# The end of a gradient kernel that is bound by transfers: the last tile's load without a wait and in one piece, its result in four pieces

## Chip, cores, metric

The kernel runs on one core of a Trainium2 chip. The metric is the device time of one execution in microseconds (us), the median of several runs. The profile is that of one execution; its span is some 2 us shorter than the time.

## The reference

```python
def setup_inputs():
    return {"x": np.random.randn(8192, 8192).astype(np.float32)}

def reference(x):
    return np.gradient(x, axis=1)
```

Inside a row every result is half the difference of the two neighbours; at the two ends it is the one-sided difference. 268.44 MB are read and as much is written.

## The kernel before

A tile is 256 rows: 128 partitions with two rows (R = 2) of 8192 values each, 64 KB per partition, 8.39 MB in all. There are 32 tiles (numbers 0 to 31) and three slots (NB = 3) for them. SP issues the loads, ScalarE the stores of tiles 0 to 30, SP the two stores of tile 31. GpSimd saves the end differences, VectorE computes in place (the result lies 64 values to the left of the input in the same slot), VectorE or ScalarE puts the ends in.

```python
def load(i):
    k = i % NB
    if i < NB:
        parts = [(ld[k], 0, R)]
    else:
        nc.sync.wait_ge(ld[(i - 1) % NB], 16 * ld_n[(i - 1) % NB])   # the load in front
        nc.sync.wait_ge(st[k], 16 * st_n[k])                         # the slot is free
        parts = [(ld[k], 0, R)] if i < nsets - 1 else [(ld_rows[r], r, 1) for r in range(R)]
    for sem, r0, nr in parts:
        nc.sync.dma_start(
            out=slots[k][:, SH + r0 * m : SH + (r0 + nr) * m],
            in_=x_sets[i, :, r0 * m : (r0 + nr) * m],
        ).then_inc(sem, 16)
    ld_n[k] += 1
...                                                                  # put_aside, work: cut
for i in range(NB):
    load(i)
for i in range(nsets):
    k = i % NB
    if i < nsets - 1:
        ready = put_aside(i, 0, R, ld[k], 16 * ld_n[k])
        placer = nc.scalar if i % 2 else nc.vector
        work(i, 0, R, ready, placer, nc.scalar, st[k])
        st_n[k] += 1
    else:                                                            # the last tile, row by row
        for r in range(R):
            ready = put_aside(i, r, 1, ld_rows[r], 16)
            work(i, r, 1, ready, nc.vector, nc.sync, st_rows[r])
    if i + NB < nsets:
        load(i + NB)
```

## Time and profile before

| | before |
|---|---|
| time, first three runs | 1249.37 us (1248.43 to 1249.98) |
| span of the profiled execution | 1246.3 us |
| bytes moved | 536.87 MB |
| VectorE busy | 554.4 us, 44% |
| the 16 DMA engines | busy without a hole until the last packets |

The page cuts the span into 40 slices; in each, the DMA row gives the busy share of the DMA engines in tenths and the row below it their rate. A transfer consists of packets, which the trace records one by one with queue, size, start and duration. Here a packet is one contiguous run of one partition: 65,536 bytes for a full tile (128 packets, eight on each engine, 2.418 us each), 32,768 bytes for one row (1.213 us). The records do not name the engine, but their number in flight at any moment does for this argument: 16 means that all engines work (the mean from 4 to 1242 us is 16.0). At the end of each transfer come 16 packets of 4 bytes, which I call the reports of the engines (1056 of them for the 66 transfers of this profile). The engine that waits for a tile goes on some 0.4 us after the last of the 16 (tile 30: reports from 1172.1 to 1176.1, GpSimd at 1176.5; second row of tile 31: last report at 1222.2, GpSimd at 1222.6). Queue q1 is SP's, q10 is ScalarE's. The lines themselves are in the prediction below.

One correction to it in advance: the times that the prediction reads from packet records (not those from the profile's own views) are 0.24 us too late, because I aligned the two clocks by hand. One reading is off by more: the first of the 16 engines is through at 1242.3, not at 1242.9, so the last packets end over 2.0 us and not over 1.7.

### The profile page before, as it was taken

Reading aid. Unit: us, or ns where it says so; the run is one execution under the profiler, and the core shown is the slowest. Engines: PE = TensorE matmul, PEld = TensorE weight load, DVE = VectorE, ACT = ScalarE, POOL = GpSimd, SP = SyncE. Lnnn points to the kernel's source line nnn. Section 1 sums busy time; section 2 is a strip of 40 time slices with the busy share of each in tenths; the row PEclk is TensorE's granted clock in tenths of the full one; section 3 lists DMA queues with packets and bytes.
Section 4 is the critical chain, followed back from the end, with each engine's and each line's share of the span. In section 5 each row is a group of like instructions: output and inputs, shape, how many; then the busy total and the mean of one; then the engine's idle time right before and its main releaser. Section 6 shows DMA issues by size and latency. Waiting matters only on the chain.

```text
span 1246.3 us, 254 instructions
## 1 busy us (share of the span) xinstructions
DVE 554.4 (44%) x51; ACT 4.2 (0%) x16; POOL 6.7 (1%) x37
## 2 busy tenths in 40 slices
DVE  2841552355533455333553345543355433554362
ACT  0000000000000000000000000000000000000000
POOL 0000000000000000000000000000000000000000
DMA  9999999999999999999999999999999999999998
GB/s 404 438 433 421 425 438 435 435 433 438 435 438 435 431 423 433 431 438 438 438 435 438 438 427 427 427 433 435 438 435 423 438 435 433 429 435 427 433 427 379
DMA packets 9504, 536.88 MB, mean 431 GB/s; under 512 B 1056, under 2 KB 1056, under 8 KB 1056
## 3 DMA queue, kind: packets, MB, share of 16 engines
q1 hardware_dynamic: 5040, 276.83, 51.6%
q10 hardware_dynamic: 4464, 260.05, 48.2%
HBM read 268.44 MB, written 268.44 MB: 431 GB/s over the span
## 4 chain that ended last, share of the span: by engine, by line
DMA 97%; DVE 2%; issue 0%; POOL 0%; SPq 0%
DMA slot<-in_x_dram 93%; DMA out_dram<-slot 3%; DVE slot L102 2%; POOL ends L84 0%; DVE slot L116 0%; SPq L72 0%; SPq L167 0%; SPq L69 0%; SPq L42 0%
## 5 line engine op out<-in xcount | busy, mean ns | idle before, releaser
L102 DVE CUSTOM_DVE_ANT_0 slot<-slot 128x16382 f32<-128x16382 f32 (+1 forms) x33 | 551.3, 16706 | 676.7 <-POOL ends L84 676.7
L84 POOL TENSOR_TENSOR ends<-slot 128x4 f32<-128x4 f32 (+1 forms) x33 | 6.5, 198 | 1215.8 <-DMA slot<-in_x_dram 1215.8
L116 ACT COPY slot<-ends 128x4 f32<-128x4 f32 x15 | 3.0, 197 | 1110.2 <-DVE slot L102 1110.2
L116 DVE COPY slot<-ends 128x4 f32<-128x4 f32 (+1 forms) x18 | 3.1, 172 | 0.6
L116 ACT ACT_TABLE_LOAD x1 | 1.3, 1283 | 41.0 <-DVE slot L116 41.0
L156 POOL MEMSET const-bfloat16-1.0<- 128x1 bf16 x1 | 0.1, 101 | 0.0
L156 POOL MEMSET const-uint8-127<- 128x1 uint8 x1 | 0.1, 101 | 0.0
L156 POOL MEMSET const-float32-0.0<- 128x1 f32 x1 | 0.1, 98 | 0.2 <-issue 0.2
L156 POOL MEMSET const-float32-1.0<- 128x1 f32 x1 | 0.1, 98 | 0.0
## 6 DMA issues: line engine op xcount, KB each, us to landing
slot<-in_x_dram SPq DMA_DIRECT2D x2, 4096.0 KB, 32.5
out_dram<-slot SPq DMA_DIRECT2D x2, 4096.0 KB, 21.4
slot<-in_x_dram SPq DMA_DIRECT2D x31, 38.6
out_dram<-slot ACTq DMA_DIRECT2D x31, 37.7
```

The source lines that it names most:

```text
L84: nc.gpsimd.tensor_sub(out=ends[:, i, r0 : r0 + nr, :], in0=xin[:, :, 1 : m : m - 2], in1=xin[:, :, 0 : m - 1 : m - 2],),
L102: nc.vector._custom_dve(dve_ops.TENSOR_TENSOR_REDUCE_SUB_MAX, out=mid, in0=after, in1=before, s0=0.0, s1=0.5,),
L116: at = done(copy(out=to, in_=of), placed[placer])
L156: nc = _bacc.Bacc("TRN2", target_bir_lowering=False, num_devices=1)
```

## The change

The intent: the last load should not wait for the load in front of it, only for its slot; in one piece it has large packets; and four small pieces let the first store start early after the landing and keep the last one short.

```diff
@@ load(i)
-            if i < NB:
-                parts = [(ld[k], 0, R)]
-            else:
-                nc.sync.wait_ge(ld[(i - 1) % NB], 16 * ld_n[(i - 1) % NB])
+            if i >= NB:
+                if i < nsets - 1:
+                    nc.sync.wait_ge(ld[(i - 1) % NB], 16 * ld_n[(i - 1) % NB])
                 nc.sync.wait_ge(st[k], 16 * st_n[k])
-                parts = [(ld[k], 0, R)] if i < nsets - 1 else [(ld_rows[r], r, 1) for r in range(R)]
-            for sem, r0, nr in parts:
-                nc.sync.dma_start(...).then_inc(sem, 16)
+            nc.sync.dma_start(out=slots[k][:, SH : SH + W], in_=x_sets[i]).then_inc(ld[k], 16)
@@ main loop, last tile
-                for r in range(R):
-                    ready = put_aside(i, r, 1, ld_rows[r], 16)
-                    work(i, r, 1, ready, nc.vector, nc.sync, st_rows[r])
+                step = W // PIECES            # PIECES = 2 * R
+                for q in range(PIECES):
+                    c0, c1 = q * step, (q + 1) * step
+                    row, right = divmod(q, 2)
+                    at = halve(b, c0 + 1 - right, c1 - right, at)
+                    edge = c1 - 1 if right else c0
+                    put = place(nc.scalar, b[:, edge : edge + 1], ends[:, i, row, right : right + 1], at)
+                    store(nc.sync, i, c0, c1, put, st_last[q])
```

(Cut: work() is split into halve, place and store with the same instructions; the ends of the last tile are put in by ScalarE instead of VectorE; the final waits name four semaphores instead of two.)

More of the change, by code (lines that the diff above doesn't have):

```diff
@@ L31 @@
     W = R * m
+    PIECES = 2 * R
     nsets = n // (P * R)
@@ L44 @@
         st = [nc.alloc_semaphore(f"st{k}") for k in range(NB)]
-        ld_rows = [nc.alloc_semaphore(f"ld_row{r}") for r in range(R)]
-        st_rows = [nc.alloc_semaphore(f"st_row{r}") for r in range(R)]
+        st_last = [nc.alloc_semaphore(f"st_last{q}") for q in range(PIECES)]
         aside = [nc.alloc_semaphore("aside"), 0]
@@ L63, in load, with put_aside @@
             k = i % NB
-            if i < NB:
-                parts = [(ld[k], 0, R)]
-            else:
-                nc.sync.wait_ge(ld[(i - 1) % NB], 16 * ld_n[(i - 1) % NB])
+            if i >= NB:
+                if i < nsets - 1:
+                    nc.sync.wait_ge(ld[(i - 1) % NB], 16 * ld_n[(i - 1) % NB])
                 nc.sync.wait_ge(st[k], 16 * st_n[k])
-                parts = [(ld[k], 0, R)] if i < nsets - 1 else [(ld_rows[r], r, 1) for r in range(R)]
-            for sem, r0, nr in parts:
-                nc.sync.dma_start(
-                    out=slots[k][:, SH + r0 * m : SH + (r0 + nr) * m],
-                    in_=x_sets[i, :, r0 * m : (r0 + nr) * m],
-                ).then_inc(sem, 16)
+            nc.sync.dma_start(out=slots[k][:, SH : SH + W], in_=x_sets[i]).then_inc(ld[k], 16)
             ld_n[k] += 1
-        def put_aside(i, r0, nr, sem, count):
+        def put_aside(i):
             k = i % NB
-            xin = slots[k][:, SH + r0 * m : SH + (r0 + nr) * m].rearrange("p (t m) -> p t m", m=m)
-            nc.gpsimd.wait_ge(sem, count)
+            xin = slots[k][:, SH : SH + W].rearrange("p (t m) -> p t m", m=m)
+            nc.gpsimd.wait_ge(ld[k], 16 * ld_n[k])
             return done(
                 nc.gpsimd.tensor_sub(
-                    out=ends[:, i, r0 : r0 + nr, :],
+                    out=ends[:, i, :, :],
                     in0=xin[:, :, 1 : m : m - 2],
@@ L90, in put_aside, with halve @@
             )
-        def work(i, r0, nr, ready, placer, storer, sem):
-            b = slots[i % NB]
-            c0, c1 = r0 * m + 1, (r0 + nr) * m - 1
-            mid = b[:, c0:c1]
-            after = b[:, SH + c0 + 1 : SH + c1 + 1]
-            before = b[:, SH + c0 - 1 : SH + c1 - 1]
+        def halve(b, c0, c1, ready):
             nc.vector.wait_ge(*ready)
-            at = done(
+            return done(
                 nc.vector._custom_dve(
                     dve_ops.TENSOR_TENSOR_REDUCE_SUB_MAX,
-                    out=mid,
-                    in0=after,
-                    in1=before,
+                    out=b[:, c0:c1],
+                    in0=b[:, SH + c0 + 1 : SH + c1 + 1],
+                    in1=b[:, SH + c0 - 1 : SH + c1 - 1],
                     s0=0.0,
@@ L111, in work, with place, store @@
             )
-            res = b[:, r0 * m : (r0 + nr) * m].rearrange("p (t m) -> p t m", m=m)
-            to, of = res[:, :, 0 : m : m - 1], ends[:, i, r0 : r0 + nr, :]
-            placer.wait_ge(*at)
-            copy = nc.scalar.copy if placer is nc.scalar else nc.vector.tensor_copy
-            at = done(copy(out=to, in_=of), placed[placer])
-            storer.wait_ge(*at)
-            storer.dma_start(
-                out=out_sets[i, :, r0 * m : (r0 + nr) * m],
-                in_=b[:, r0 * m : (r0 + nr) * m],
-            ).then_inc(sem, 16)
+        def place(engine, out, in_, ready):
+            engine.wait_ge(*ready)
+            copy = nc.scalar.copy if engine is nc.scalar else nc.vector.tensor_copy
+            return done(copy(out=out, in_=in_), placed[engine])
+        def store(engine, i, c0, c1, ready, sem):
+            engine.wait_ge(*ready)
+            engine.dma_start(out=out_sets[i, :, c0:c1], in_=slots[i % NB][:, c0:c1]).then_inc(sem, 16)
         for i in range(NB):
@@ L126 @@
             k = i % NB
+            b = slots[k]
+            at = put_aside(i)
             if i < nsets - 1:
-                ready = put_aside(i, 0, R, ld[k], 16 * ld_n[k])
-                placer = nc.scalar if i % 2 else nc.vector
-                work(i, 0, R, ready, placer, nc.scalar, st[k])
+                at = halve(b, 1, W - 1, at)
+                rows = b[:, 0:W].rearrange("p (t m) -> p t m", m=m)
+                at = place(nc.scalar if i % 2 else nc.vector, rows[:, :, 0 : m : m - 1], ends[:, i, :, :], at)
+                store(nc.scalar, i, 0, W, at, st[k])
                 st_n[k] += 1
             else:
-                for r in range(R):
-                    ready = put_aside(i, r, 1, ld_rows[r], 16)
-                    work(i, r, 1, ready, nc.vector, nc.sync, st_rows[r])
+                step = W // PIECES
[6 more added lines that the diff above has]
+                    store(nc.sync, i, c0, c1, put, st_last[q])
             if i + NB < nsets:
                 load(i + NB)
-        for r in range(R):
-            nc.sync.wait_ge(st_rows[r], 16)
         for k in range(NB):
             nc.sync.wait_ge(st[k], 16 * st_n[k])
+        for q in range(PIECES):
+            nc.sync.wait_ge(st_last[q], 16)
 _INS = ['x']
```

## The prediction

> **What bounds the kernel now.** I read the page of the profile first, its DMA rows and its chain, then the waits of the SP queue, then a table of the last 100 us stretch by stretch, and last the queues in two of those stretches. The page, its two DMA rows and the chain:
>
> ```profile
> span 1246.3 us, 254 instructions
> DVE 554.4 (44%) x51; ACT 4.2 (0%) x16; POOL 6.7 (1%) x37
> ...
> DMA  9999999999999999999999999999999999999998
> GB/s 404 438 433 421 425 438 435 435 433 438 435 438 435 431 423 433 431 438 438 438 435 438 438 427 427 427 433 435 438 435 423 438 435 433 429 435 427 433 427 379
> ...
> DMA 97%; DVE 2%; issue 0%; POOL 0%; SPq 0%
> ```
>
> The 16 DMA engines are 90% busy or more in every slice but the last, and the chain that ends last is DMA for 97%. VectorE works 44% of the span. 536.87 MB have to move at some 434 GB/s: 1237 us of the 1246.3. What is left for everything else, start and end included, is about 9 us. The change touches only the last of 32 tiles, so the question is whether the DMA engines stand idle anywhere near the end. The SP queue does wait for long, and on what the change removes:
>
> ```profile
> SPq L69 <- DMA out_dram<-slot: 587.5, 29, 79.6
> SPq L72 <- DMA slot<-in_x_dram: 576.0, 28, 21.9
> ```
>
> The second line is the wait for the load in front, up to 21.9 us at a time. A waiting queue is not an idle DMA engine, though. The table by stretch (columns: stretch and length in us; busy us of VectorE, ScalarE, GpSimd; clock; DMA share; GB/s):
>
> ```profile
> 1174.00:1178.00 4.00, 1.22 (x1) 0.00 (x0) 0.20 (x1) 1.00 0.94 410
> 1178.00:1190.00 12.00, 12.00 (x1) 0.00 (x0) 0.00 (x0) 1.00 0.95 412
> 1190.00:1196.00 6.00, 4.18 (x2) 0.00 (x0) 0.01 (x1) 1.00 1.01 437
> 1196.00:1205.00 9.00, 8.75 (x2) 0.00 (x0) 0.18 (x1) 1.00 1.09 470
> 1205.00:1220.00 15.00, 0.11 (x1) 0.00 (x0) 0.00 (x0) 1.00 1.01 435
> 1220.00:1225.00 5.00, 2.19 (x1) 0.00 (x0) 0.19 (x1) 1.00 0.85 367
> 1225.00:1235.00 10.00, 6.67 (x2) 0.00 (x0) 0.00 (x0) 1.00 0.97 419
> 1235.00:1242.00 7.00, 0.00 (x0) 0.00 (x0) 0.00 (x0) 1.00 1.04 449
> 1242.00:1246.30 4.30, 0.00 (x0) 0.00 (x0) 0.00 (x0) 1.00 0.13 53
> ```
>
> Each transfer piece is put down to the stretch in which it starts, hence shares over 1 and the 0.85. Cutting each piece at the stretch's edges in the trace's packet records gives 16.0 engines busy in every 3 us from 4 us after the start up to 1242. So there is no hole before the very end: the last pieces end between 1242.9 and 1244.6 on the different engines, the last landing is at 1244.6, and 1.7 us of ending follow. Now the queue that the removed wait empties, from 1171 to 1181 (q1 is SP's queue, q10 ScalarE's), and the stretch from 1205 to 1220 in which the last half-load lies beside the store of tile 30:
>
> ```profile
> q10 hardware_dynamic: 60, 3.93, 90.7%
> q1 hardware_dynamic: 23, 0.26, 6.2%
> ...
> q10 hardware_dynamic: 74, 4.85, 75.7%
> q1 hardware_dynamic: 63, 1.67, 25.8%
> ```
>
> In the first pair q1 is almost empty and q10 takes 91% of the engines: the hole that the wait makes in one queue is filled by the other. In the second pair both queues have work, but q1's pieces are half as large (32,768 bytes, a row of one partition) as q10's (65,536 bytes), and q1 gets about a quarter.
>
> [...]with equal packets (1155 to 1174) each queue moved 4.19 MB, with 32 KB against 64 KB packets 1.67 against 4.85. [...]the steady slices show 433 to 438. [...]17,224 ns at N=16382[...] and 8,690 at 8190[...], so I take an estimate of 4.43 us for the new quarter pieces.
>
> **The change part by part.**
>
> *Removed: the wait for load 30.* Load 31 is issued at 1176.5 now, when load 30 has landed. Its slot is free when store 28 has landed, at 1154.5, so it will be issued some 22 us earlier. It does not move earlier by 22 us: load 30 is ahead of it in the same queue, with data until 1170.0 to 1174.0. It follows directly, at about 1172, where its first packets now start at 1180.8 to 1182.7. So 9 to 10 us of q1's emptiness go. The DMA engines gain nothing from it, since q10 used that time: store 29 loses it and becomes later.
>
> *Replaced: two half-loads by one.* Packets of 64 KB against 64 KB give the last load a half of the engines instead of a third or a quarter. Working in packets of 2.42 us per engine (8 per engine and full tile): at 1172 store 29 has 3 of its 8 done (q10 had 7.35 us of engine time from 1158 to 1173, over 2.42). Its other 5 alternate with load 31 until 1172 + 10 x 2.42 = 1196. Store 30 is issued at 1194.2 as now and needs about 4 us to its first packet (1137.75 to 1141.8 at load 30), so load 31 gets about one more alone; its last 2 alternate with store 30 until 1198.3 + 4 x 2.42 = 1208. One packet turn until the semaphore (2.42 us lie between last data and landing wherever the other queue is busy) and about 2 us for the slowest engine: the load lands at about 1212.5, against 1222.4 now. Ten microseconds earlier for the last tile's data.
>
> *Compute in four pieces.* GpSimd 0.2, VectorE 4.43, ScalarE copy 0.2 and four hand-overs: the first piece is issued at about 1217.4, the others every 4.46 us after: 1221.9, 1226.4, 1230.8. VectorE works 17.8 us after the landing instead of 8.7, but not on the path: see the next part.
>
> *Stores.* At 1208 store 30 has 6 packets to go, alone: until 1208 + 6 x 2.42 = 1222.5. The first piece is in the ring by about 1219 to 1221, so the engines go over without a hole, with 1.5 to 3.5 us to spare. A quarter piece is 8 packets of 16 KB per engine. From 1,213 ns for 32 KB and 2,418 for 64 KB I get some 8 ns fixed per packet, thus an estimate of 0.61 us each, 4.9 us a piece. The pieces are eaten from 1222.5, 1227.4, 1232.3 and 1237.2 and supplied before that each time. End of data: 1222.5 + 4 x 4.9 = 1242.1. The same count for the kernel before (store 30 and both half-stores, 16 packets of 1.213) gives 1172 + 21 x 2.42 + 19.4 = 1242.2, against 1242.9 to 1244.6 measured.
>
> The sum: bytes are the same, the engines are full in both kernels, and smaller packets cost 16 x 0.008 = 0.13 us. One DMA and some waits more are issued off the path. What could be won at all is the unevenness of the last packets, 1.7 us between first and last engine, less than 1 us on average. I expect a gain between 0 and 0.5 us.
>
> **The rivals.** (1) *The removed wait was a real loss.* Anyone reading the chain sees load, wait, load, and q1 empty for 9 to 10 us; filled at half rate that would be worth 5 us, a time of 1244. Against it: 16.0 engines busy throughout that gap. (2) *The tail becomes compute-bound.* If load 31 landed no earlier than now (1222.5), the fourth piece would be issued at 1222.5 + 18.3 = 1240.8; with some 1.5 us to its first packet, 4.9 us of data and the ending of 1.7, the span is about 1249 and the time 1252. In favour: twice the VectorE time after one landing, instead of a row computed while the other arrives. Against: one-piece packets win back their share. The landing could slip to about 1217 before the last piece comes late. (3) *Small pieces starve beside big ones.* 16 KB against 64 KB gives the pieces a fifth while store 30 runs. True, but nobody loses: whoever is served, the bytes are served, and store 30 is not needed earlier. (4) *Finer pieces even out the engines' ends,* 0.5 to 1 us gained, time 1248.5.
>
> **Range and chances.** The three times of before lie between 1248.43 and 1249.98, median 1249.37, with no cause but chance; the same spread and perhaps another chip go with the new kernel. Base: -0.3 us from the tail, so 1249.0. Rival 2 or a small hole puts it up to 1251, rival 4 and half of rival 1 down to 1247. Range 1247.4 to 1250.8. Two per cent are 25 us; no step here can move a fifth of that, so within 2% has a chance of 0.99, the rest split.
>
> **What would show it right or wrong.** The DMA row still at 9 throughout with the last slice at 8 or 9; the load of the last tile issued near 1154.5 and the last GpSimd subtraction at about 1212 to 1216 instead of 1222.6; in 1171 to 1181 the two queues near half and half; store 29 landing near 1198 instead of 1189.8; store 30 ending within 5 us of where it does now (1227.6 landing); VectorE's four pieces of 4.4 us back to back, followed by a wait of SP for the last store of some 10 us. I am wrong if the engines are idle between store 30's end and the first piece, if the last tile lands after 1218, or if the span falls by more than 2 us: then the gap that the wait made cost something that the packet records do not show.

Cut from it, at the marks, are rules that no trace or run of this case shows; the measured numbers that stood beside them remain. The two times are those of VectorE's custom operation at 16382 and 8190 elements. For a quarter piece a straight line through these two times gives 4.42 us.

Two delays in it are estimates: 1.6 to 3.6 us from the issue of the first piece until it is "in the ring" (it means: ready for the engines), and 1.5 us from the issue of the last piece to its first packet (rival 2). In the profile before, issue to first packet was 3.5 to 4.5 us for loads 3 to 31 (of the last, its first row) and 1.26 us for the last half-store (1231.73 to 1232.99). And the 2.42 us between last data and landing hold beside 64 KB packets, not "wherever the other queue is busy": for tile 30 2.41 us (data until 1169.7 to 1173.7 on the different engines, reports 1172.1 to 1176.1), but for store 29, beside 32 KB packets, 1.2 us (1185.4 to 1188.3, 1186.6 to 1189.5).

## The result, and the profile after

| | before | after |
|---|---|---|
| median of six runs | 1249.58 us (1247.92 to 1254.9) | 1249.33 us (1248.0 to 1250.94) |
| ratio of fast runs | | 0.9995, 95% interval 0.9975 to 1.0014 |
| span profiled | 1246.3 us | 1247.0 us |

A ratio is the mean time of one kernel's fast runs over that of the other's of the same rounds, so it is not quite the ratio of the medians.

The page of the changed kernel (span; busy us by engine; DMA row and rate in 40 slices):

```profile
span 1247.0 us, 258 instructions
DVE 554.4 (44%) x51; ACT 5.0 (0%) x20; POOL 6.5 (1%) x36
...
DMA  9999999999999999999999999999999999999998
GB/s 404 437 437 435 420 423 437 437 435 437 435 437 437 435 429 425 429 433 433 433 437 437 437 431 437 423 431 429 433 435 429 433 435 435 437 431 433 423 429 376
```

The DMA row is the same digit for digit; the last slice has 376 GB/s after 379. The waits of the SP queue (waiter, awaited, us in total, times, longest):

```profile
SPq L71 <- DMA slot<-in_x_dram: 549.3, 27, 22.2
...
SPq L71 <- DMA out_dram<-slot: 16.5, 1, 16.5
SPq L139 <- DMA out_dram<-slot: 10.3, 3, 4.8
```

The wait for the load in front is there 27 times instead of 28 and 27 us shorter in sum. Some 22 us of this are the wait that went (1154.6 to 1176.5 before); the rest differs between the two executions. The span did not follow. The new line, 16.5 us once, is the last load's wait for its slot; it was issued at 1155.9. The two queues from 1171 to 1181, the stretch in which q1 was empty before (packets, MB, share of 16 engines):

```profile
q10 hardware_dynamic: 37, 2.42, 55.9%
q1 hardware_dynamic: 39, 1.77, 40.9%
```

Before, q10 had 91% and q1 6%. The emptiness of one queue is gone, the engines move the same (4.19 MB in both). Now the tail, instruction by instruction (start, us, engine, line, operation, output and input, count, idle time before). First the kernel before, whose two half-stores are issued from 1205.1 on:

```profile
1205.13 26.94 SPq L118 DMA_DIRECT2D out_dram<-slot  x2
1222.58 0.19 POOL L84 TENSOR_TENSOR ends<-slot 128x2 f32<-128x2 f32 x1 [26.40 <-DMA slot<-in_x_dram]
1222.81 8.69 DVE L102 CUSTOM_DVE_ANT_0 slot<-slot 128x8190 f32<-128x8190 f32 x1 [17.70 <-POOL ends L84]
```

Then the changed kernel:

```profile
1216.52 0.20 POOL L80 TENSOR_TENSOR ends<-slot 128x4 f32<-128x4 f32 x1 [38.46 <-DMA slot<-in_x_dram]
1216.75 17.80 DVE L92 CUSTOM_DVE_ANT_0 slot<-slot 128x4095 f32<-128x4095 f32 x4 [21.23 <-POOL ends L80]
1221.21 0.19 ACT L106 COPY slot<-ends 128x1 f32<-128x1 f32 x1 [64.44 <-DVE slot L92]
1221.43 13.71 SPq L110 DMA_DIRECT2D out_dram<-slot  x4
```

The GpSimd line marks the landing of the last data: 1222.6 before, 1216.5 after. VectorE then works 17.8 us instead of 8.7. The last store is issued at 1231.7 before and at 1234.8 after. Six microseconds came earlier at one place and three later at another, and both lie beside full DMA engines: from 1220 on (stretch and length; busy us of VectorE, ScalarE, GpSimd; clock; DMA share; GB/s):

```profile
1220.00:1225.00 5.00, 4.97 (x2) 0.19 (x1) 0.00 (x0) 1.00 0.90 347
1225.00:1235.00 10.00, 9.49 (x3) 0.57 (x3) 0.00 (x0) 1.00 1.01 431
1235.00:1242.00 7.00, 0.00 (x0) 0.00 (x0) 0.00 (x0) 1.00 1.00 428
```

As before, a packet counts where it starts; cut at the edges, 16 engines are busy until 1243.4. Store 30's packets end between 1223.2 and 1225.8 on the different engines, the first piece's start at 1223.2 on the first of them: no hole. The spare time was small, though: the first piece was issued at 1221.4, and 0.84 us lay between issue and first packet where the engines were free (one_store: 1232.05 to 1232.89; two_pieces: 1227.3 to 1228.1), which leaves 0.9 us.

### The profile page after: what moved, and what is told of

Read it like the earlier page. It is cut to its first block, busy times and chain, and to the rows that moved or that the text cites. A ratio compares the mean times of both kernels' runs of the same rounds, so it can differ in the third digit from the quotient of the medians.

```text
span 1247.0 us, 258 instructions
## 1 busy us (share of the span) xinstructions
DVE 554.4 (44%) x51; ACT 5.0 (0%) x20; POOL 6.5 (1%) x36
## 4 chain that ended last, share of the span: by engine, by line
DMA 93%; another core or an unknown queue 3%; DVE 3%; issue 0%; POOL 0%; ACT 0%; SPq 0%
DMA slot<-in_x_dram 90%; DMA out_dram<-slot 3%; DVE slot L92 3%; POOL ends L80 0%; ACT slot L106 0%; DVE slot L106 0%; SPq L165 0%; SPq L70 0%; SPq L45 0%
## 5 line engine op out<-in xcount | busy, mean ns | idle before, releaser
L80 POOL TENSOR_TENSOR ends<-slot 128x4 f32<-128x4 f32 x32 | 6.3, 198 | 1209.9 <-DMA slot<-in_x_dram 1209.9
L106 ACT COPY slot<-ends 128x4 f32<-128x4 f32 (+1 forms) x19 | 3.7, 196 | 1188.7 <-DVE slot L92 1188.7
L106 DVE COPY slot<-ends 128x4 f32<-128x4 f32 x16 | 2.8, 172 | 0.6
```

What stands on the lines that cost most here:

```text
L80: nc.gpsimd.tensor_sub(out=ends[:, i, :, :], in0=xin[:, :, 1 : m : m - 2], in1=xin[:, :, 0 : m - 1 : m - 2],),
L106: return done(copy(out=out, in_=in_), placed[engine])
```

## A balance for all the runs

Before the experiments, the instrument by which they are read. From the packet records I add up, for the 16 engines together and divided by 16: **holes** (engines idle between 1170 and the last moment at which all 16 work), the **uneven end** (engines idle from then until the last packet ends), the **slow packets** (what packets took above 2.418, 1.213, 0.611 or 0.309 us for 64, 32, 16, 8 KB), and the **ending** after the last packet. "Rest" is the span less these four. (The kept_wait profile, a slow execution, is left out.)

| profiled execution | span | holes | uneven end | slow packets | ending | rest |
|---|---|---|---|---|---|---|
| before | 1246.3 | 0.0 | 1.2 | 4.6 | 1.9 | 1238.6 |
| after | 1247.0 | 0.0 | 1.1 | 5.4 | 1.8 | 1238.7 |
| after_again | 1251.8 | 1.5 | 3.1 | 6.8 | 1.8 | 1238.6 |
| kept_wait_2 | 1249.0 | 0.2 | 2.5 | 5.5 | 2.2 | 1238.6 |
| rows_no_wait | 1251.0 | 3.2 | 1.4 | 6.1 | 1.7 | 1238.6 |
| rows_no_wait_2 | 1256.7 | 8.6 | 0.1 | 7.6 | 1.7 | 1238.7 |
| rows_four | 1255.5 | 4.3 | 2.9 | 7.3 | 2.3 | 1238.7 |
| rows_both | 1246.8 | 0.1 | 2.1 | 4.3 | 1.7 | 1238.6 |
| one_store | 1254.1 | 11.3 | 0.1 | 2.4 | 1.7 | 1238.6 |
| late_load | 1249.3 | 2.9 | 0.4 | 5.2 | 2.2 | 1238.6 |
| two_pieces | 1249.5 | 2.6 | 0.1 | 6.5 | 1.7 | 1238.6 |
| eight_pieces | 1248.5 | 0.0 | 2.4 | 5.1 | 2.2 | 1238.8 |
| no_waits | 1249.0 | 0.0 | 6.0 | 2.6 | 1.7 | 1238.7 |

The rest is 1238.6 to 1238.8 us for every program: start and bytes. This is bookkeeping, since all move the same bytes; what it tests is that no holes lie before 1170. All differences in span lie in the four columns. Holes (0.0 to 11.3 us) and uneven end (0.1 to 6.0 us) are what the programs changed. The slow packets are nearly all packets of loads (4.3 of 4.6 us before, 4.9 of 5.4 after). 1.4 to 1.9 us of them lie in the first 80 us of every execution, 0.7 to 5.0 between 80 and 1170, where all programs but no_waits do the same work, so that these are differences between executions; after 1170 it is 0.0 to 1.1 us but for rows_four (1.7) and late_load (2.7), to which I come back.

## The experiments

My theory: transfers are the bound, one queue's gap is filled by the other, and an edit of the tail counts only by the holes it opens or closes. Main rival: the removed wait was a real gain (3 to 5 us) which the small pieces gave back. The runs came in four calls, each on another chip and with its own runs of the kernel before.

**kept_wait: the changed kernel with the wait put back**

```diff
-                if i < nsets - 1:
-                    nc.sync.wait_ge(ld[(i - 1) % NB], 16 * ld_n[(i - 1) % NB])
+                nc.sync.wait_ge(ld[(i - 1) % NB], 16 * ld_n[(i - 1) % NB])
```

> The changed kernel with the wait for load 30 put back; one-piece load and four pieces stay. My theory (the DMA engines are full in either case, the other queue uses the gap): load 31 is issued near 1177, starts near 1181 with 64 KB packets at half share, store 29 lands near 1190 instead of 1199.7, and the last tile lands at 1214 to 1217, not later than in the changed kernel (1216.4); time within 1 us of both kernels, ratio 1.000. Rival (the removed wait was a real gain that the four pieces gave back): the load lands 8 to 10 us later, near 1226, and the time is 3 to 5 us above the changed kernel's, near 1253.

Ratio 0.999 (0.9972 to 1.0008), fast runs 1246.41 to 1249.54 us. The rival's 3 to 5 us are excluded. The profile of this run is useless: it fell in a single execution of 1336 us, and no conclusion is drawn from it. So it was run again:

> The changed kernel with the wait for load 30 kept, again, because the profile of its first look was a single slow execution. My theory: ratio 1.000 again, last tile landing at 1214 to 1217, store 29 near 1190, engines full to the last packets. Rival: the load lands near 1226 and the time is 3 us or more above the changed kernel.

Ratio 0.9982 (0.9965 to 0.9999), median 1250.09 us. The landings of tiles 30 and 31, as GpSimd's lines show them in this kernel:

```profile
1179.55 0.20 POOL L79 TENSOR_TENSOR ends<-slot 128x4 f32<-128x4 f32 x1 [38.44 <-DMA slot<-in_x_dram]
1218.19 0.20 POOL L79 TENSOR_TENSOR ends<-slot 128x4 f32<-128x4 f32 x1 [38.44 <-DMA slot<-in_x_dram]
```

and in the changed kernel, the line before the one shown above:

```profile
1177.86 0.20 POOL L80 TENSOR_TENSOR ends<-slot 128x4 f32<-128x4 f32 x1 [38.58 <-DMA slot<-in_x_dram]
```

With the wait the last tile lands 38.64 us after the one in front, without it 38.66 us; in the kernel before it was 46.0 (1222.58 less 1176.55). So in these profiles, one of each kernel, the earlier landing is not owed to the removed wait: the one-piece load did it alone. With the wait store 29 lands earlier (1196.4 instead of 1199.6, in spans that are not shifted alike), and what the load loses at its beginning it gets back, as I read it, while q10 is empty after that store (store 30 is issued at 1197.2).

**rows_no_wait: the other half of the change, the wait removed from the kernel before, its two-row load kept**

```diff
-                nc.sync.wait_ge(ld[(i - 1) % NB], 16 * ld_n[(i - 1) % NB])
+                if i < nsets - 1:
+                    nc.sync.wait_ge(ld[(i - 1) % NB], 16 * ld_n[(i - 1) % NB])
```

> The kernel before with only the wait for load 30 taken away from its last load; that load stays in two half-row packets and the last tile in two pieces. My theory: q1 no longer empties, the second row lands near 1217 instead of 1222.4, nothing moves at the end: ratio 1.000, time 1249 to 1250, engines full until the last packets. Rival (the wait cost, the pieces gave it back): 3 to 5 us faster, near 1245.

Ratio 1.0068 (1.0014 to 1.0123), median 1255.32 against 1249.96 us. Neither theory had this: the removal alone costs 5 us by the medians. The profile shows a hole ahead of the last half-store, and, from 1201 to 1212, how the last row shares the engines with store 30:

```profile
1233.50:1238.00 4.50, 3.58 (x2) 0.00 (x0) 0.00 (x0) 1.00 0.27 117
```

```profile
q10 hardware_dynamic: 48, 3.15, 66.2%
q1 hardware_dynamic: 48, 1.57, 33.7%
```

Packets alternate one for one, 48 and 48, so the 64 KB queue gets two thirds, 66.2%. GpSimd went on at 1228.0, when the slowest of the 16 engines was done (1227.6). The times at which the 16 engines reported (the 4-byte packets of the records, in us):

```text
                        the leaders        the last three
tile 30                 1171.1 to 1171.4   1175.5 1175.6 1180.2
tile 31, first row      1195.2 to 1195.6   1199.1 1199.5 1200.5
tile 31, second row     1212.1 to 1212.5   1223.9 1226.4 1227.6
```

Three engines enter the last load 4 to 9 us late. The leaders move many of their 32 KB packets while q10 is empty; the late ones have more of them left when store 30 arrives, and each then costs 2.42 + 1.21 us instead of 1.21. (That is read from the durations and the even count; in the kernel before, the 32 KB packets beside store 30 do come 3.6 us apart: the foremost start at 1200.0, 1203.6, 1207.4, 1211.0 and 1214.6.) A delay of 4 to 5 us becomes one of 12 to 15. The second row landed at 1227.9, its store was issued at 1237.1, and 13 of 16 engines had run out of the first half-store at 1234. In the kernel before, with the wait, all engines begin the last load within 2 us (first packets 1180.6 to 1182.5), and the second row's reports spread over 6.5 us only (1215.7 to 1222.2). That the wait is what kept the engines together is argued and not shown by this: one engine was already 8.6 to 9.0 us behind the first at tile 29 in both slow profiles (rows_no_wait and its repeat), before the edit could act, against 4.2 in the kernel before; and in kept_wait_2, with the wait, the last load's first packets lie within 1.9 us, but its reports spread over 8.7 us. Even in the kernel before the half-stores joined without a gap only just: the first one's packets end at 1233.0 on the fastest engine, and there the second's begin.

It was run again, to see whether this was chance:

> The kernel before without the wait for load 30, again: was the 5 us loss of the first time chance? Theory: its 13 leading engines had landed the last row at 1212 and three stragglers only at 1224 to 1228, since each 32 KB packet left when store 30 starts waits behind a 64 KB one; the last half-store was then issued at 1237, after the first half-store had run out at 1234. If so it is again slower than before, by 2 to 8 us, with a hole on most engines ahead of the last half-store. Rival (chance): ratio 1.000 within 0.002 and no hole.

Ratio 1.004 (1.0026 to 1.0055), median 1256.75 against 1252.29 us, all four runs between 1256.08 and 1258.85. Not chance. One engine alone reported the second row at 1234.7, the next at 1223.4, the others by 1219.7, and the hole is larger:

```profile
1235.00:1245.00 10.00, 8.86 (x2) 0.00 (x0) 0.20 (x1) 1.00 0.10 43
```

The balance has 8.6 us of holes for it. The difference in time is smaller than that; the uneven end is 0.1 instead of 1.2 us, and the kernel before was itself slower on this chip (1252.29), where no profile of it was taken.

**rows_four: is the loss in the load or in the two large pieces?** The slow version with the last tile computed and stored in four half-row pieces.

```diff
                 for r in range(R):
                     ready = put_aside(i, r, 1, ld_rows[r], 16)
-                    work(i, r, 1, ready, nc.vector, nc.sync, st_rows[r])
+                    for right in range(2):
+                        half_row(i, r, right, ready, st_rows[2 * r + right])
```

(half_row: a half-row by VectorE, its end by ScalarE, its store by SP. Each VectorE instruction waits for the one before, as it works in place.)

> The last load without the wait and in two rows, as in the run before, but computed and stored in four half-row pieces as in the changed kernel. If the loss came from the last piece being ready too late, four pieces close the hole: the third piece is ready 4.4 us earlier than a whole row, so 3 to 5 us faster than the two-row version, near 1250, although the last row still lands late (1222 to 1228). If the loss lies in the load itself (half-row packets, stragglers), it stays, near 1255.

Ratio 1.0031 (1.0012 to 1.005), median 1256.71 us, runs from 1252.55 to 1257.77. The loss stays. The second row landed at 1234.1, the third piece was issued at 1239.1, and the holes are 4.3 us. So smaller pieces do not mend a late landing of this size; the loss lies in the load. On the same chip the changed kernel (after_again, below), which also has four pieces and no wait but a load in one piece, took 1251.45 us.

**rows_both: equal packets.** The slow version, with the store of tile 30 cut into two rows too, so that 32 KB stand against 32 KB.

```diff
-            storer.dma_start(out=..., in_=...).then_inc(sem, 16)
+            cuts = [(r0, nr)] if i != nsets - 2 else [(r, 1) for r in range(R)]
+            for q0, nq in cuts:
+                storer.dma_start(out=..., in_=...).then_inc(sem, 16)
```

> The slow version (last load without the wait, in two rows of 32 KB packets), but the store of tile 30, which runs beside the second row, is cut into two rows too, so that its packets are 32 KB as well. If the stragglers come from 32 KB packets taking turns with 64 KB ones (a third of the engine for the load), equal packets give the load half: the straggling engines land no more than 5 to 9 us behind the leaders, the last row lands by about 1222 instead of 1228 to 1235, the last half-store is issued before 1233, the hole ahead of it goes, and the time is within 2 us of the kernel before. Rival (the loss comes from the missing wait itself, through engines out of step, whatever the packets): still 4 to 6 us slower than before, with the row landing after 1226.

Ratio 1.0005 (0.9963 to 1.0047), median 1250.01 against 1250.54 us. The interval is wide, as the kernel before ran unevenly here (1246.55 to 1254.48 and one slow run of 1325.17, which is left out), but the hole is gone from the profile. From 1201 to 1212, and the stretch in which the hole was:

```profile
q10 hardware_dynamic: 78, 2.56, 53.8%
q1 hardware_dynamic: 74, 2.16, 45.6%
```

```profile
1233.00:1238.00 5.00, 0.00 (x0) 0.00 (x0) 0.00 (x0) 1.00 0.97 419
```

In this execution eight engines landed tile 30 some 4 us after the others (1175.4 to 1175.8 against 1171.0 to 1171.4), so a lag was there again, though not the 9.1 and 7.6 us that the last engine had in the two slow profiles. This time it did not grow: the second row's reports lie at 1209.0 to 1209.3 and 1212.1 to 1214.8. It landed at 1215.2, and the last half-store was issued at 1224.4. My reading: the missing wait lets engines stay out of step, and unequal packets turn that into a late landing. The loss came only where both were present: in rows_no_wait, its repeat and rows_four, but not with the wait (before) nor with equal packets (after, after_again, rows_both). Two things stay open: the interval of rows_both alone reaches 1.0047, past the 1.004 of the second slow run, and how the wait acts is not shown, as said above.

**one_store: no pieces at all.** The last tile is treated as every other one (the else branch is deleted).

> The changed kernel with the last tile computed and stored whole, as the other tiles. My theory: the last tile still lands near 1216.4; VectorE 17.2 us and hand-overs put its store at about 1234.3, first packet near 1236; store 30 ends at 1223.6 to 1226.1, so the engines stand idle for some 11 us, then 19.3 us of data: span about 1257.5, time about 1260, +10 us, ratio 1.008. Rival (small pieces cost as much as they bring): within 1 us of the changed kernel.

Ratio 1.0063 (1.0048 to 1.0078), median 1257.1 against 1249.96 us. The rival of this run is excluded: without pieces the kernel is slower. The hole:

```profile
1221.00:1233.00 12.00, 10.79 (x1) 0.20 (x1) 0.00 (x0) 1.00 0.20 87
```

It is 11.3 us, as expected, yet the time grew by 7.1 and not by 10. The balance says where 4 us went in the profiled execution: the hole swallowed the uneven end (0.1 us instead of 1.1: the last store's packets end between 1252.3 and 1252.4 on all engines), and the slow packets were 2.4 us instead of 5.4. 11.3 - 1.0 - 3.0 = 7.3, against 7.1 in the spans. Whether the slow packets of the other three runs were as few is not known, so that part of the shortfall stays open.

**late_load: a longer wait instead of none**

```diff
                 if i < nsets - 1:
                     nc.sync.wait_ge(ld[(i - 1) % NB], 16 * ld_n[(i - 1) % NB])
+                else:
+                    nc.sync.wait_ge(st[(i - 2) % NB], 16 * (st_n[(i - 2) % NB] + 1))   # store 29
```

> The changed kernel with a longer wait in front of the last load: it waits for store 29 instead of for nothing. My theory says that a wait costs only where both queues are empty at once: store 29 lands near 1188, the load's first packets come near 1190, after a hole of 3 to 4 us in which neither queue has data; the load lands near 1224, store 30 ends near 1229, the first piece's packets come near 1231, a second hole of about 2 us: 5 to 7 us more, time near 1255, ratio 1.005. Rival (the 22 us that the load starts earlier are worth half of themselves): this load starts another 12 us later than with the old wait, so 10 us or more above the changed kernel, near 1260.

Ratio 1.0029 (1.0012 to 1.0046), median 1252.96 against 1249.96 us. Here a wait does cost, since both queues are empty at once:

```profile
1182.00:1186.00 4.00, 4.00 (x1) 0.00 (x0) 0.00 (x0) 1.00 0.46 147
```

The hole is 2.9 us. Store 29 landed at 1184.7, sooner than I thought, and the load had the engines to itself until 1197, so that it landed at 1219.9 instead of near 1224; the second hole that I expected is not there (store 30 ends from 1226.4 to 1226.8, the first piece's packets start from 1226.4 to 1226.8). The load was issued 29 us later than in the changed kernel (1184.7 against 1155.9) and that cost 3 us by the medians. The hole is not all that the delay cost in the profiled execution: 33 packets of this load, started at 1185.7 to 1186.3 and at 1193.8 to 1199.4, took more than 2.5 us instead of 2.418, some of them up to 4.2, which adds 2.0 us of slow packets; the earlier part of this execution had fewer of them than the changed kernel's, and its end was more even. So in this execution the late load cost through its slow packets too. Why they are slow there stays open.

**two_pieces and eight_pieces: how many pieces it takes**

```diff
-    PIECES = 2 * R
+    PIECES = R          # two_pieces, both ends of a row placed by one copy; eight_pieces: 4 * R
```

> The changed kernel with the last tile in two pieces of a row each (the load stays whole and early). My theory: landing near 1216.4, first piece issued near 1225.8, its first packets near 1227.2, store 30 ends at 1223.6 to 1226.1: a hole of 1 to 3 us, so 1 to 3 us slower than the changed kernel, near 1251.5. Rival (small pieces cost): as fast or faster than the changed kernel.

> The changed kernel with eight pieces of a quarter row. My theory: the engines are full with four already, so nothing is won; 8 KB packets cost an estimated 0.2 us more: time 1249 to 1250, ratio to the changed kernel 1.000. Rival (packets this small are slow, or issuing and completing them limits): 1 us or more slower.

Two pieces: median 1252.02 against 1250.61 us, ratio 1.0004 (0.9981 to 1.0027). The times decide nothing, as the kernel before had runs up to 1258.19. The profile has the expected hole, 2.6 us in the balance, between the end of store 30 (1224.7 to 1227.3) and the first packets of the first piece (1228.1):

```profile
1224.00:1228.00 4.00, 3.97 (x2) 0.19 (x1) 0.00 (x0) 1.00 0.19 82
```

Eight pieces: median 1251.0 us, ratio 0.9997 (0.997 to 1.0023), no hole. Four suffice, and more bring nothing. (The 0.2 us of the expectation is an estimate; by the packets' medians 64 of 8 KB, at 0.309 us, take 0.22 us longer per engine than 32 of 16 KB, at 0.611.)

**no_waits: the wait for the load in front removed everywhere**

```diff
-                if i < nsets - 1:
-                    nc.sync.wait_ge(ld[(i - 1) % NB], 16 * ld_n[(i - 1) % NB])
```

> The changed kernel with the wait for the load in front taken from all loads, not only the last. Theory 1 (bytes): the engines were never idle, so nothing changes: ratio 1.000 within 0.001. Theory 2 (slow packets): in both profiled kernels about 4.5 us per engine are lost in single load packets that take longer than 2.42 us, and they lie mostly where a queue starts again after having run empty; with neither queue ever empty most of 3.5 us of that goes away: 2 to 3 us faster, near 1247, ratio 0.998, and the load packets' mean falls from 2437 towards 2425 ns. Theory 3: loads that pile up hold the stores back and the time grows by more than 3 us.

Ratio 1.0024 (0.998 to 1.0068): too wide to tell the theories apart. Its five fast runs lie between 1246.14 and 1260.96 us (a sixth, 1270.25, counts as slow and is left out), against 1248.48 to 1258.19 for the eleven of the kernel before. The second theory of this run, that the slow packets would go, looks confirmed at first (2.6 us instead of 5.4, load packets' mean 2428 ns). It is not: one_store kept all the waits but the last and has 2.4 us and 2427 ns. What sets them stays open. (Where they lie, as the expectation says, is shown: after the first 80 us, 93% of the load packets' excess over 2.418 us in the profile before and 77% in the one after lies in packets that start at most 3 us after the first packet of a transfer of either queue, or during which such a first packet starts; 31% and 32% of the load packets are of that kind.) What the profile does show is the engines out of step: store 29's 16 reports spread over 12 us (1194.0 to 1206.1), and at the end one engine works alone until 1247.3 while the others were through between 1240 and 1243.3, an uneven end of 6.0 us against 1.1. That the wide spread of the times comes from this is likely, but one profile of one run does not show it.

**after_again: the changed kernel a second time, beside the slow versions**

> The changed kernel once more, so that it shares a chip and rounds with the three below: ratio 1.000, 1249 to 1251 us, spread of its runs under 3 us.

Ratio 0.9997 (0.9981 to 1.0013), median 1251.45 against 1252.29 us, four runs from 1249.72 to 1253.99, wider than expected. The profiled execution was the longest of them and had one engine about 3 us behind the rest: the last tile landed at 1221.3, one engine's report (1220.9) coming 5.8 us after the next, and 1.5 us of holes opened ahead of the first piece. So the changed kernel has the same weak spot, with a smaller effect. Two of the signs by which the prediction said it would be wrong (a landing after 1218, engines idle ahead of the first piece) are there in this execution.

No version beats both kernels by more than the noise. kept_wait comes nearest (0.999 and 0.998, the second interval ending at 0.9999), and I would not call that shown.

## Why the prediction was right, point by point

- **The bound.** Right. The balance gives the same 1238.6 to 1238.8 us for start and bytes in all 13 profiled executions, and between the first profiles of the two kernels the edit changed neither holes nor that. (The prediction calls slices of 433 to 438 GB/s steady; but for the first and the last, all slices lie between 421 and 438.)
- **The removed wait.** The step said that q10 had used the gap. Right, and shown by kept_wait and kept_wait_2. The step also let the last load win time from its earlier start. That was wrong: with and without the wait it lands 38.6 us after tile 30.
- **Large packets for the last load.** Right in kind: half the engines instead of a third (after, 1178 to 1194: 48 packets of q1 beside 51 of q10, 45.3% against 48.2%). (The quarter that the prediction reads mixes two states: from 1202 to 1213 both queues moved 48 packets, one for one, 33.1% against 67.0%, and later the row was through on some engines.) The landing was put at 1212.5 and came at 1216.5. The load started on the different engines from 1172.6 to 1177.4, not all at 1172, and one engine reported at 1216.1, 2.4 us after all the others; the 2 us allowed for the slowest were too few. So the margin ahead of the first piece was 0.9 us instead of the 1.5 to 3.5 us claimed, and in after_again it was gone.
- **Pieces.** VectorE 4.43 us each estimated, 4.425 measured; 16 KB packets 0.61 us estimated, 0.611 median, 0.627 mean. The last packets were put at 1242.1 and ended at 1243.4 to 1245.2. The sum for the end starts all engines at 1172 and allows for no lag between them. Its 0.13 us for smaller packets forgets that the load has eight packets fewer per engine; with them it is half of that.
- **Rivals.** (1), the wait as a loss: excluded by kept_wait and kept_wait_2. (2), a tail bound by compute: not in this kernel, but right as a mechanism, and nearer than I gave it: with two pieces 2.6 us of holes appear, with one 11.3. (3), starving small pieces: not shown for stores, as the pieces' first packets came only when store 30 was ending (1223.2 to 1225.8), so the fifth stays an estimate from the packets' durations; but the same unequal sharing applied to a load (33.7% against 66.2%) is, by my reading above, what makes rows_no_wait slow, and the prediction did not think of that case. (4), more even ends: no, 1.1 us against 1.2.
- **The size.** 1249.0 predicted, 1249.33 measured. The agreement to 0.3 us is luck, given runs that spread over 3 us; that the two kernels are equal is not.

## What to carry to other kernels

A long wait of one queue cost nothing here, where the other queue kept the DMA engines full (22 us of it, with ratios of 0.999 and 0.998 to the kernel before when it was put back into the changed one); before removing such a wait, count engines in flight, not waits. At the end of a transfer-bound kernel ask what stands in the queues between the last landing and the first store after it, and cut the last piece of work so small that the store in front covers it (here 0.0 us of holes with four pieces in the first profile, 2.6 with two, 11.3 with one). Give transfers that run side by side packets of the same size, above all when one of them is awaited: with 32 KB against 64 KB the awaited load had a third of the engines (33.7% in rows_no_wait; 45.6% with 32 KB on both sides in rows_both), and engines that were 4 to 5 us late with its first row were 12 to 15 us late with its second. Look at all 16 reports of an awaited load: those of the second row spread over 15.4 us (1212.1 to 1227.6) in rows_no_wait and over 18.7 us (1216.0 to 1234.7) when it was repeated. And profile more than once: the hole of after_again (1.5 us) is not in the first profile of the same kernel.
